# Copying two PSUM banks with one ScalarE instruction, from tiles two banks wide and four deep

## The chip, the cores and the metric

The kernel runs on one core of one Trainium2 chip. The metric is the device time of one execution in microseconds, the median of several runs. In the profiles PE is TensorE (the matmuls), DVE is VectorE, ACT is ScalarE, SP is the engine whose queue issues the transfers, and "PEclk" is the granted TensorE clock. A profile's span is about 1.8 us shorter than the timed execution.

## The reference

```python
batch, m, k, n = 16, 512, 768, 1024
x: [batch, k, m] float32      y: [batch, k, n] float32

def reference(x, y):
    return np.einsum('bkm,bkn->bmn', x, y).astype(np.float32)
```

Sixteen products of a transposed 768x512 matrix with a 768x1024 one. Each batch reads 1536 KB of x and 3072 KB of y and writes 2048 KB.

## The kernel before

For each batch the kernel loads x and y in float32, casts both to bfloat16 on VectorE, multiplies in 48 matmuls of 128x512 (4 row blocks `mo`, 2 column halves `nt`, 6 steps `kt` over K), lets ScalarE copy each finished PSUM bank into an output tile, and stores a whole batch with one transfer. Loads and stores share one queue. A batch's store is issued four batches late (`LAG = 4`), behind the loads of a later batch, so that it never waits for its data in the middle of the kernel. The last batch loads y in two halves, and keeps all its accumulations open while it goes through K in two passes.

```python
o_pool = ctx.enter_context(tc.tile_pool(name="o_pool", bufs=5))
psum = ctx.enter_context(tc.tile_pool(name="psum", bufs=8, space=bass.MemoryType.PSUM))
LAG = 4
# ...
for b in range(B):
    # ... loads of xs and ys; halves = 2 for the last batch, else 1
    if b >= LAG:
        store(b - LAG)
    # ... casts to x_sb, y_sb
    for h in range(halves):
        for mo in range(MT):
            for nt in range(NT):
                if h == 0:
                    ps[mo, nt] = psum.tile([P, NF], FP32, name="ps")
                for kt in range(h * KT // halves, (h + 1) * KT // halves):
                    mm(ps[mo, nt], x_w, y_sb, kt, mo, nt)
                if h == halves - 1:
                    nc.scalar.copy(o_sb[:, mo, nt * NF:(nt + 1) * NF], ps[mo, nt][:])
for b in sorted(o_tiles):      # the last four stores
    store(b)
```

Of the kernel before, what the change touches and what calls it, by code (L numbers as in the profile page):

```python
# [1 line left out]

_os.environ.setdefault("NEURON_RT_ULTRASERVER_MODE", "4")

# [1 line left out]

# [4 lines left out]


@with_exitstack
def kernel(
    ctx: ExitStack,
    tc: tile.TileContext,
    x: bass.AP,
    y: bass.AP,
    out: bass.AP,
):  # L20
    nc = tc.nc
    P = 128
    FP32 = mybir.dt.float32
    BF16 = mybir.dt.bfloat16

    B, K, M = x.shape
    _, _, N = y.shape
    KT = K // P
    MT = M // P
    NF = 512  # L30
    NT = N // NF



    x_v = x.rearrange("b (p ko) m -> b p ko m", ko=KT)
    y_v = y.rearrange("b (p ko) n -> b p ko n", ko=KT)
    o_v = out.rearrange("b (p mo) n -> b p mo n", mo=MT)

    xs_pool = ctx.enter_context(tc.tile_pool(name="xs_pool", bufs=2))
    ys_pool = ctx.enter_context(tc.tile_pool(name="ys_pool", bufs=2))  # L40
    x_pool = ctx.enter_context(tc.tile_pool(name="x_pool", bufs=2))
    y_pool = ctx.enter_context(tc.tile_pool(name="y_pool", bufs=2))
    o_pool = ctx.enter_context(tc.tile_pool(name="o_pool", bufs=5))
    psum = ctx.enter_context(tc.tile_pool(name="psum", bufs=8, space=bass.MemoryType.PSUM))
    LAG = 4
    KH = KT // 2
    o_tiles = {}

    def load(dst, src, rows):
        nc.sync.dma_start(dst, src)  # L50

    def store(b):
        nc.sync.dma_start(o_v[b], o_tiles.pop(b)[:])

    def mm(ps, x_w, y_sb, kt, mo, nt):
        nc.tensor.matmul(ps[:], x_w[:, kt, mo], y_sb[:, kt, nt * NF:(nt + 1) * NF],  # L56
                         start=(kt == 0), stop=(kt == KT - 1))

    with tc.manual_schedule():

        for b in range(B):
            xs = xs_pool.tile([P, KT, M], FP32, name="xs")
            ys = ys_pool.tile([P, KT, N], FP32, name="ys")
            halves = 2 if b == B - 1 else 1

            load(xs[:], x_v[b], 1)
            for h in range(halves):
                ks = slice(h * KT // halves, (h + 1) * KT // halves)
                load(ys[:, ks], y_v[b, :, ks], 1)

            if b >= LAG:
                store(b - LAG)
            x_sb = x_pool.tile([P, KT, M], BF16, name="x_sb")
            y_sb = y_pool.tile([P, KT, N], BF16, name="y_sb")
            nc.vector.tensor_copy(x_sb[:], xs[:])  # L75
            for h in range(2):
                ks = slice(h * KH, (h + 1) * KH)
                nc.vector.tensor_copy(y_sb[:, ks], ys[:, ks])  # L78
            x_w = x_sb[:].rearrange("p k (j mo) -> p k mo j", mo=MT)
            o_sb = o_pool.tile([P, MT, N], FP32, name="o_sb")  # L80
            o_tiles[b] = o_sb
            ps = {}


            for h in range(halves):
                for mo in range(MT):
                    for nt in range(NT):
                        if h == 0:
                            ps[mo, nt] = psum.tile([P, NF], FP32, name="ps")
                        for kt in range(h * KT // halves, (h + 1) * KT // halves):  # L90
                            mm(ps[mo, nt], x_w, y_sb, kt, mo, nt)
                        if h == halves - 1:
                            nc.scalar.copy(o_sb[:, mo, nt * NF:(nt + 1) * NF], ps[mo, nt][:])  # L93
        for b in sorted(o_tiles):
            store(b)


# [1 line left out]
_INS = ['x', 'y']  # L99
_OUTS = [((16, 512, 1024), 'float32')]  # L100


# [23 lines left out]
```

## Time and profile before

The time was 262.4 us in three runs.

| What | Before |
|---|---|
| span of the profile | 260.5 us |
| share of the 16 DMA engines used by the one queue | 98.4% |
| TensorE / VectorE / ScalarE busy | 73% / 32% / 29% |
| rate in the middle, 95 to 220 us | 431 GB/s |
| last copy ends | 245.65 us |
| DMA engines stay full until about | 256 us |

The lines behind this table are shown and read in the prediction.

### The profile page before, as it was taken

The page shows a single profiled execution, that of the slowest core. Times are in us where ns is not written, and L with a number is a line of the kernel's source. Part 1 is how long each engine was busy: PE and PEld are TensorE (multiplying, and loading weights), DVE is VectorE, ACT ScalarE, POOL GpSimd, SP SyncE. Part 2 cuts the span into 40 slices and gives each one's busy share as a digit, 9 for nine tenths or more (in the row PEclk, how much of TensorE's full clock was granted, in tenths as well). Part 3 has the DMA queues.
Part 4 walks back from the last instruction along what each step waited for, and adds up shares of the span by engine and source line. Part 5 has one row for each costly group of instructions (what it writes and reads, how often), then busy time and mean ns, then how long its engine had stood idle before and what let it go on. Part 6 is the DMA issues. An engine that isn't in the chain of part 4 may idle for free.

```text
span 260.5 us, 1879 instructions
## 1 busy us (share of the span) xinstructions
PE 191.3 (73%) x768; PEld 89.3 (34%) x768; DVE 83.1 (32%) x48; ACT 76.4 (29%) x129; POOL 0.2 (0%) x4
## 2 busy tenths in 40 slices
PE   0049999897939959688496966969789395899600
PEld 0014555453513514334142432434335142355200
DVE  0271633525222252322524214252132522252000
ACT  1003444442421403324032330323314043141600
POOL 0000000000000000000000000000000000000000
PEclk9999999999985977979898896797979889799955
DMA  7999999999999999999999999999999999999994
GB/s 279 434 434 411 445 423 436 426 387 420 446 416 442 423 422 455 409 440 418 438 435 415 453 418 431 423 428 449 410 443 421 426 445 407 431 430 430 435 428 201
DMA packets 7065, 109.18 MB, mean 419 GB/s; under 512 B 784, under 2 KB 784, under 8 KB 784
## 3 DMA queue, kind: packets, MB, share of 16 engines
q1 hardware_dynamic: 7056, 109.06, 98.4%
q8 instruction: 6, 0.10, 0.1%
q14 instruction: 3, 0.02, 0.0%
HBM read 75.50 MB, written 33.55 MB: 419 GB/s over the span
## 4 chain that ended last, share of the span: by engine, by line
DMA 74%; DVE 11%; PE 8%; issue 0%; ACT 0%; SPq 0%; DVEq 0%
DMA ys<-in_y_dram 74%; DVE y_sb L78 11%; PE ps L56 8%; ACT o_sb L93 0%; SPq L50 0%; DVEq L78 0%
## 5 line engine op out<-in xcount | busy, mean ns | idle before, releaser
L56 PE MATMUL ps<-y_sb,x_sb 128*128 128x512 bf16 x768 | 191.3, 412 | 53.8 <-DVE y_sb L78 53.8
L56 PEld LDWEIGHTS <-x_sb 128*128 128x128 bf16 x768 | 89.3, 118 | 155.2 <-issue 45.9
L93 ACT COPY o_sb<-ps 128x512 f32<-128x512 f32 x128 | 75.1, 587 | 168.6 <-PE ps L56 168.2
L78 DVE CAST y_sb<-ys 128x3072 bf16<-128x3072 f32 x32 | 55.0, 1757 | 87.4 <-DMA ys<-in_y_dram 87.4
L75 DVE CAST x_sb<-xs 128x3072 bf16<-128x3072 f32 x16 | 28.2, 1760 | 66.6 <-DMA xs<-in_x_dram 60.4
L93 ACT ACT_TABLE_LOAD x1 | 1.3, 1283 | 0.7 <-PEq L110 0.7
L110 POOL MEMSET const-bfloat16-1.0<- 128x1 bf16 x1 | 0.1, 101 | 0.0
L110 POOL MEMSET const-uint8-127<- 128x1 uint8 x1 | 0.1, 101 | 0.0
L110 POOL MEMSET const-float32-0.0<- 128x1 f32 x1 | 0.1, 98 | 0.2 <-issue 0.2
L110 POOL MEMSET const-float32-1.0<- 128x1 f32 x1 | 0.1, 98 | 0.0
## 6 DMA issues: line engine op xcount, KB each, us to landing
ys<-in_y_dram SPq DMA_DIRECT2D x15, 3072.0 KB, 28.1
out_dram<-o_sb SPq DMA_DIRECT2D x16, 2048.0 KB, 32.6
xs<-in_x_dram SPq DMA_DIRECT2D x16, 1536.0 KB, 29.7
ys<-in_y_dram SPq DMA_DIRECT2D x2, 1536.0 KB, 26.1
```

Of the source, the lines that this page charges most:

```text
L56: nc.tensor.matmul(ps[:], x_w[:, kt, mo], y_sb[:, kt, nt * NF:(nt + 1) * NF], start=(kt == 0), stop=(kt == KT - 1))
L75: nc.vector.tensor_copy(x_sb[:], xs[:])
L78: nc.vector.tensor_copy(y_sb[:, ks], ys[:, ks])
L93: nc.scalar.copy(o_sb[:, mo, nt * NF:(nt + 1) * NF], ps[mo, nt][:])
L110: nc = _bacc.Bacc("TRN2", target_bir_lowering=False, num_devices=1)
```

## The change

The intent is to pay the fixed part of a ScalarE instruction once for two banks. A PSUM tile becomes two banks wide, the pool four deep instead of eight (the same eight banks), and 64 copies of 1024 columns take the place of 128 copies of 512. The rest of the diff takes small helper functions apart and changes no instruction; it is cut here.

```diff
-    psum = ctx.enter_context(tc.tile_pool(name="psum", bufs=8, space=bass.MemoryType.PSUM))
+    psum = ctx.enter_context(tc.tile_pool(name="psum", bufs=4, space=bass.MemoryType.PSUM))
 ...
                 for mo in range(MT):
+                    if h == 0:
+                        ps[mo] = psum.tile([P, NT, NF], FP32, name="ps")
                     for nt in range(NT):
-                        if h == 0:
-                            ps[mo, nt] = psum.tile([P, NF], FP32, name="ps")
                         for kt in range(h * KT // halves, (h + 1) * KT // halves):
-                            mm(ps[mo, nt], x_w, y_sb, kt, mo, nt)
-                        if h == halves - 1:
-                            nc.scalar.copy(o_sb[:, mo, nt * NF:(nt + 1) * NF], ps[mo, nt][:])
+                            nc.tensor.matmul(
+                                ps[mo][:, nt], x_w[:, kt, mo],
+                                y_sb[:, kt, nt * NF:(nt + 1) * NF],
+                                start=(kt == 0), stop=(kt == KT - 1))
+                    if h == halves - 1:
+                        nc.scalar.copy(o_sb[:, mo].rearrange("p (t f) -> p t f", f=NF), ps[mo][:])
```

More of the change, by code (lines that the diff above doesn't have):

```diff
@@ L47 @@
     o_tiles = {}
-    def load(dst, src, rows):
-        nc.sync.dma_start(dst, src)
     def store(b):
-        nc.sync.dma_start(o_v[b], o_tiles.pop(b)[:])
-    def mm(ps, x_w, y_sb, kt, mo, nt):
-        nc.tensor.matmul(ps[:], x_w[:, kt, mo], y_sb[:, kt, nt * NF:(nt + 1) * NF],
-                         start=(kt == 0), stop=(kt == KT - 1))
+        o_sb = o_tiles.pop(b)
+        nc.sync.dma_start(o_v[b], o_sb[:])
     with tc.manual_schedule():
@@ L64 @@
             halves = 2 if b == B - 1 else 1
-            load(xs[:], x_v[b], 1)
+            nc.sync.dma_start(xs[:], x_v[b])
             for h in range(halves):
                 ks = slice(h * KT // halves, (h + 1) * KT // halves)
-                load(ys[:, ks], y_v[b, :, ks], 1)
+                nc.sync.dma_start(ys[:, ks], y_v[b, :, ks])
             if b >= LAG:
```

## The prediction

> **What bounds the kernel now.** I read the page first, then the chain of waits, the timeline of the end and of one middle batch, the windows over the last microseconds, and the waits of the DMA queue. The first question is which resource has no holes.
>
> ```profile
> PE   0049999897939959688496966969789395899600
> ACT  1003444442421403324032330323314043141600
> PEclk9999999999985977979898896797979889799955
> DMA  7999999999999999999999999999999999999994
> ...
> q1 hardware_dynamic: 7056, 109.06, 98.4%
> ...
> DMA ys<-in_y_dram 74%; DVE y_sb L78 11%; PE ps L56 8%; ACT o_sb L93 0%; SPq L50 0%; DVEq L78 0%
> ```
>
> From the page: the DMA row is 9 in every slice except the first and the last, and the one queue accounts for 98.4% of what 16 engines could do. The chain of work that ended last is 74% the y load and only a rounded 0% ScalarE's copy. TensorE has holes, and ScalarE, the engine that the change relieves, is never above six tenths.
>
> The size of a period fits. A batch moves 1536 KB of x, 3072 KB of y and 2048 KB of output, 6656 KB or 6.82 MB. In the timeline the y loads of successive batches are issued at 127.86, 143.68 and 159.56 us, 15.85 us apart. 6.82 MB in 15.85 us is 430 GB/s, which is what the windows view shows for the long middle stretch (95 to 220 us: 431 GB/s at full DMA share). So the middle of the kernel runs at the rate of the transfers. All 109.06 MB at 430 GB/s would be 253.6 us. The span is 260.5 us; the rest is the start, the ragged end of the last store (below), and slightly slower stretches.
>
> Next, does anything wait for ScalarE?
>
> ```profile
> ACT o_sb L93 <- PE ps L56: 168.2, 121, 17.4
> DVE y_sb L78 <- DMA ys<-in_y_dram: 87.4, 17, 6.8
> DVE x_sb L75 <- DMA xs<-in_x_dram: 60.4, 14, 7.1
> PE ps L56 <- DVE y_sb L78: 53.8, 25, 16.2
> ```
>
> In this list of waits (total us, times, longest) ScalarE waits for TensorE 121 times; TensorE waits for VectorE's cast, and VectorE for the loads. TensorE never appears as waiting for ScalarE. In the DMA queue's own list of waits ScalarE appears only three times, 32.2 us in all, before stores, and the timeline places these at the very end, where the last stores wait for the last batches to be computed.
>
> **What the Trainium skill says.** (1) "ScalarE: Activation LUTs", section What ACT_TABLE_LOAD costs: an activation without pointer operands costs 186 ns plus 0.833 ns per element. For 512 elements that gives 613 ns; the trace has 587 ns, 4% less. (2) "Perfetto Trace Analysis", section Optimizing Scalar/DVE Operations: grouping into larger operations helps throughput if the engine is saturated. At 29% busy, ScalarE is not, so the condition for a gain is missing. (3) "PSUM — Partial Sum Buffer", section PSUM bank collisions raise a hardware error: guard PSUM by bank; a reader and TensorE must not be in one bank together. A two-bank tile therefore keeps both banks from TensorE until the one wide copy is done; whether that costs time is worked out below. (4) "DMA: Bandwidth & Descriptors", Specifications: a fabric ceiling of 435 GB/s for the 16 engines. The steady 430 GB/s is 99% of it, which agrees, so no reordering of compute can make the middle faster.
>
> **The change, part by part.** The loads, casts, matmuls, stores and their order stay as they are: dropping the small helper functions changes no instruction, and the store pieces are still whole 2048 KB batches on the same queue. Two things move.
>
> ```profile
> L93 ACT COPY o_sb<-ps 128x512 f32<-128x512 f32 x128 | 75.1, 587 | 168.6 <-PE ps L56 168.2
> L56 PE MATMUL ps<-y_sb,x_sb 128*128 128x512 bf16 x768 | 191.3, 412 | 53.8 <-DVE y_sb L78 53.8
> ```
>
> *Fewer, wider copies.* 128 copies of 512 columns become 64 of 1024. Keeping the page's slope and taking the fixed part from the trace, 587 - 0.833 x 512 = 160 ns, a wide copy should take 160 + 853 = 1.01 us (estimate). ScalarE's copies fall from 75.1 to 64 x 1.01 = 65 us. These 10 us lie on an engine that stood idle 168.6 us waiting for TensorE, so they are worth nothing to the end.
>
> *Later start, later end of each copy.* The first bank of a pair now waits for the second. Within a batch the timeline has copies starting every 1.30 us, six matmuls of about 0.216 us each at full clock. So the first bank is read 1.30 us later, and the pair is finished 1.01 - 0.59 = 0.43 us later than its second bank was. In the middle this delays nothing: a batch's store is issued four batches, some 63 us, afterwards.
>
> *Coarser PSUM.* A tile is filled in 12 x 0.216 = 2.6 us and emptied in 1.0. Before TensorE needs it again it fills three others, 3 x 2.6 = 7.8 us. So about 6.8 us are to spare and TensorE should not stall. At a lower clock the filling is slower and the reserve larger. The last batch goes through K in two halves, so all four tiles are open at once. It starts at mo=0 after the preceding batch's tiles; its fourth tile is first written after 3 x 1.3 = 3.9 us, while the previous batch's last copy needs 1.0. In the second half TensorE needs six matmuls, 1.30 us, per pair and ScalarE 1.01, so ScalarE still keeps up.
>
> *The end.* This is the one place where the 0.43 us can reach the clock.
>
> ```profile
> 240.58 5.07 ACT L93 COPY o_sb<-ps 128x512 f32<-128x512 f32 x8 [5.29 <-PE ps L56]
> ...
> 246.00:248.00 2.00, 0.00 (x0) 0.00 (x0) 0.00 (x0) 0.00 (x0) 0.00 (x0) 0.88 1.05 451
> 248.00:250.00 2.00, 0.00 (x0) 0.00 (x0) 0.00 (x0) 0.00 (x0) 0.00 (x0) 0.50 0.98 418
> 250.00:252.00 2.00, 0.00 (x0) 0.00 (x0) 0.00 (x0) 0.00 (x0) 0.00 (x0) 0.50 0.98 418
> 252.00:254.00 2.00, 0.00 (x0) 0.00 (x0) 0.00 (x0) 0.00 (x0) 0.00 (x0) 0.50 1.05 451
> 254.00:256.00 2.00, 0.00 (x0) 0.00 (x0) 0.00 (x0) 0.00 (x0) 0.00 (x0) 0.50 0.96 410
> 256.00:258.00 2.00, 0.00 (x0) 0.00 (x0) 0.00 (x0) 0.00 (x0) 0.00 (x0) 0.50 0.44 188
> 258.00:261.00 3.00, 0.00 (x0) 0.00 (x0) 0.00 (x0) 0.00 (x0) 0.00 (x0) 0.50 0.06 27
> ```
>
> The last copy ends at 245.65 us and the last store is issued at 245.7. The last columns of the windows are DMA share and GB/s: the engines stay full until 256. Summing rate times width, 4.75 MB move after 246.0: 4.30 up to 256, then 0.38, then 0.08. The last store is 2048 KB, 2.10 MB. So some 2.66 MB of earlier stores were still ahead of it when it was issued, and at 430 GB/s that is **6.2 us of reserve** (estimate). A delay of 0.43 us uses 7% of it. The engines don't notice, and the end stays where it was.
>
> The sum: 0 from ScalarE's saved 10 us, 0 from PSUM, 0 from the tail, and the DMA's bytes are unchanged.
>
> **The rivals.** (a) *The tail shows*: if the last store ran alone, the end would move by 0.43 us, to 262.8 us. For it: the chain ends in a copy. Against it: the reserve of 2.66 MB. Even then it would be 0.2%. (b) *TensorE becomes starved of PSUM*: four deep instead of eight. If every one of 64 tiles stalled for the extra 0.43 us of copy, this would be 28 us on TensorE. Most of it would vanish into the 53.8 us in which TensorE waits for data, but from 18 to 51 us TensorE runs almost without a gap, three batches in about the time of their loads. Stalls there could delay the casts and hence the loads, by perhaps 12 x 0.43 = 5 us. Against it: 6.8 us to spare in every rotation. (c) *ScalarE was a hidden limit and the kernel gets faster*: if its saved 10 us counted, 252 us. Against it: no engine waits for it in the listed waits, and 252 us would be below the 253.6 us that the bytes need at 430 GB/s. (d) *The wide read is much slower than 1.01 us*, say 2 x 587 ns: then ScalarE is as busy as before and the tail is 0.59 us later, still inside the reserve.
>
> **Range and chances.** The point is the time before, 262.4 us. The three runs before span 0.5 us; another chip or session may shift a transfer-bound time by a few tenths of a per cent, a judgment and not a measurement. I take 261.4 to 263.6 us. For over 2% slower (267.6 us) rival (b) at its full size would be needed, 2%. For over 2% faster (257.2 us) the transfers would have to run at more than 430 GB/s, or the start and ragged end shrink, which the change doesn't touch: 1%.
>
> **What would show it.** In the changed kernel: 64 copies of 128x1024 near 1.01 us and about 65 us in all; TensorE's waits still put down to VectorE, none to ScalarE; the DMA row unchanged, the middle at 430 GB/s and a period of 15.85 us; the last copy ending about 0.4 us after TensorE's end plus 0.6, and the stores' end unchanged. It would be wrong if TensorE shows waits for ScalarE before y loads are issued later, if the last store finds the engines empty, or if the transfers' rate moves for a reason that the page doesn't show.

## More of the kernel before

The experiments were spread over three chips, each with the kernel before in the same rounds; there it took 262.00 to 262.25 us.

## The result, and the profile after

The changed kernel took 262.13 us (261.85 to 262.35, six runs), the kernel before 262.33 us (262.04 to 262.52, six runs). The ratio is 0.9993, with a 95% interval from 0.998 to 1.0006: the same. A ratio here is the mean time of one kernel's fast runs over that of the other's in the same rounds, so it isn't quite the ratio of the medians.

From the page of the changed kernel, the answers to the lines of before: two rows of the forty slices, the queue's share, the chain by line, and the two groups that changed.

```profile
ACT  1003343433321313314033330412404114131600
...
DMA  7999999999999999999999999999999999999995
...
q1 hardware_dynamic: 7056, 109.06, 98.5%
...
DMA ys<-in_y_dram 74%; DVE y_sb L70 11%; PE ps L83 8%; ACT o_sb L88 0%; SPq L59 0%; DVEq L70 0%
...
L83 PE MATMUL ps<-y_sb,x_sb 128*128 128x512 bf16 x768 | 189.9, 410 | 55.1 <-DVE y_sb L70 55.1
...
L88 ACT COPY o_sb<-ps 128x1024 f32<-128x1024 f32 x64 | 64.9, 1014 | 179.1 <-PE ps L83 179.1
```

The copies did become cheaper: 64 of 1014 ns, 64.9 us instead of 75.1. The idle time before them grew by about as much, from 168.6 to 179.1 us. TensorE still waits for VectorE's cast only, and the DMA row and the chain haven't moved. (The chain is followed back from the last copy, so the 14 us of stores after it are not part of it.) The saved time turned into more waiting on an engine that was already waiting.

At the end of the kernel, the timeline shows the last copy and the windows show the last transfers (the last two columns are DMA share and GB/s).

```profile
244.99 1.01 ACT L88 COPY o_sb<-ps 128x1024 f32<-128x1024 f32 x1 [0.28 <-PE ps L83]
```

```profile
254.00:256.00 2.00, 0.00 (x0) 0.00 (x0) 0.00 (x0) 0.00 (x0) 0.00 (x0) 0.50 1.03 442
256.00:258.00 2.00, 0.00 (x0) 0.00 (x0) 0.00 (x0) 0.00 (x0) 0.00 (x0) 0.50 0.52 221
258.00:261.00 3.00, 0.00 (x0) 0.00 (x0) 0.00 (x0) 0.00 (x0) 0.00 (x0) 0.50 0.04 16
```

The copy takes 1.01 us where it took 0.58, and ends at 246.00 us instead of 245.65 although TensorE finished 0.08 us earlier. The transfers still end where they did. The waits of the DMA queue show how the delay vanishes. This line is the time from the issue of the last store until it landed (us in total, times, longest), first for the kernel before, then for the changed one.

```profile
SPq L121 <- DMA out_dram<-o_sb: 13.4, 1, 13.4
```

```profile
SPq L116 <- DMA out_dram<-o_sb: 13.0, 1, 13.0
```

The last store was issued 0.35 us later and its wait became 0.4 us shorter. It had been standing in line behind earlier stores, and now it stands there for less time. The first experiments test this reading.

### The profile page after: what moved, and what is told of

The parts are those of the page before. It is cut to its first block, busy times and chain, and to the rows that moved or that the text cites. A ratio compares the mean times of both kernels' runs of the same rounds, so it can differ in the third digit from the quotient of the medians.

```text
span 260.4 us, 1815 instructions
## 1 busy us (share of the span) xinstructions
PE 189.9 (73%) x768; PEld 89.1 (34%) x768; DVE 83.1 (32%) x48; ACT 66.2 (25%) x65; POOL 0.2 (0%) x4
## 3 DMA queue, kind: packets, MB, share of 16 engines
q1 hardware_dynamic: 7056, 109.06, 98.5%
## 4 chain that ended last, share of the span: by engine, by line
DMA 74%; DVE 11%; PE 8%; ACT 0%; issue 0%; SPq 0%; DVEq 0%
DMA ys<-in_y_dram 74%; DVE y_sb L70 11%; PE ps L83 8%; ACT o_sb L88 0%; SPq L59 0%; DVEq L70 0%
## 5 line engine op out<-in xcount | busy, mean ns | idle before, releaser
L88 ACT COPY o_sb<-ps 128x1024 f32<-128x1024 f32 x64 | 64.9, 1014 | 179.1 <-PE ps L83 179.1
```

Source lines behind the costliest of these rows:

```text
L88: nc.scalar.copy(o_sb[:, mo].rearrange("p (t f) -> p t f", f=NF), ps[mo][:])
```

## The experiments

My theory: the bytes at 430 GB/s set the time; ScalarE, the depth of PSUM and the last copy all have room. Rivals: the end follows the last copy; the coarser tiles cost what the wider copies save, so that two real effects cancel; ScalarE counts after all, but a wide copy isn't really cheaper. Where an experiment differs from the changed kernel, its edit is shown against that one, unless said otherwise.

### Later last store

```diff
-                        nc.scalar.copy(o_sb[:, mo]..., ps[mo][:])
+                        for _ in range(5 if b == B - 1 and mo == MT - 1 else 1):   # 5, 9, 13
+                            nc.scalar.copy(o_sb[:, mo]..., ps[mo][:])
```

> The very last wide copy is done five times instead of once, so the last store is issued 4.1 us later. Theory (when the last store is issued, some 2.6 MB of earlier stores are still ahead of it, about 6 us of reserve): the time stays at 262.1, within 0.5 us. Rival (the end follows the last copy): 266.2 us.

> The last copy nine times, the last store 8.1 us later. Theory: the reserve of about 6 us is used up and the rest shows, with perhaps 1 us more for a store that starts on empty engines: 264 to 266 us. Rival (the end follows the last copy): 270.2 us. Rival (the end does not depend on the last copy at all): 262.1 us.

> The last copy thirteen times, the last store 12.2 us later. Theory: 4.1 us more than with nine copies, so 268 to 270 us, and the profile shows the DMA engines empty between the third last store and the last. Rival (the end follows the last copy all along): 274.3 us.

Measured: 262.24 us (ratio to the kernel before 1.0005), 262.57 us (1.002) and 266.51 us (1.0177). The extra copies took 4.2, 8.4 and 12.5 us. Four were hidden completely, eight nearly so, and of twelve about 4.4 us show. That rules out "the end follows the last copy", which asked for 266.2 us in the first of these, and it rules out that the end is independent of it. But the size was not what I had written: with eight, 264 us or more was expected, and with twelve 268 to 270.

The wait for the last store to land, with eight and then with twelve extra copies:

```profile
SPq L117 <- DMA out_dram<-o_sb: 5.8, 1, 5.8
```

```profile
SPq L117 <- DMA out_dram<-o_sb: 5.8, 1, 5.8
```

So a 2048 KB store that finds the engines free takes 5.8 us to land. In the changed kernel it took 13.0. The difference, **7.2 us**, is the reserve of the changed kernel, and 13.4 - 5.8 = 7.6 us is that of the kernel before. In the run with twelve extra copies the last store was issued here:

```profile
257.39 0.33 SPq L52 DMA_DIRECT2D out_dram<-o_sb  x1
```

It was out at 257.72 us instead of 246.36 (both ends of the issuing instruction), 11.36 us later; less 7.2, that is 4.2 us, and the span grew by 4.2 us, from 260.4 to 264.6. The 5.8 us of the run with eight thus foretell the run with twelve. With four, the last store was issued 3.5 us later than in the changed kernel and its wait fell to 9.7 us, 3.3 less, as for a store that stands in a line.

Why did adding up bytes give only 6.2? The windows of the run with eight extra copies, which issued its last store at 253.56 us:

```profile
250.00:252.00 2.00, 0.00 (x0) 0.00 (x0) 0.00 (x0) 1.94 (x3) 0.00 (x0) 0.50 0.75 320
252.00:253.00 1.00, 0.00 (x0) 0.00 (x0) 0.00 (x0) 0.97 (x2) 0.00 (x0) 0.50 0.31 131
253.00:254.00 1.00, 0.00 (x0) 0.00 (x0) 0.00 (x0) 0.54 (x1) 0.00 (x0) 0.50 0.04 16
...
258.00:259.00 1.00, 0.00 (x0) 0.00 (x0) 0.00 (x0) 0.00 (x0) 0.00 (x0) 0.50 1.23 524
259.00:261.00 2.00, 0.00 (x0) 0.00 (x0) 0.00 (x0) 0.00 (x0) 0.00 (x0) 0.50 0.00 0
```

The earlier stores don't end at one time. The share, a mean of the 16 engines, falls from 0.75 to 0.04 over some three microseconds. A store that comes after that ends sharply, at 524 GB/s and then nothing. No view lists the parts of a transfer, but the trace keeps the 16 times at which each transfer reports a part as landed, and they settle it. In the kernel before, the parts of the last store landed between 256.22 and 259.63 us, 3.4 us apart; in the run with eight extra copies they landed between 259.64 and 259.83, 0.2 us apart. Counted from the end of the issuing instruction, the mean part took 11.67 us in the kernel before and 5.87 when the store stood alone, 5.8 us more; the last part took 13.62 and 5.93, 7.7 us more. Adding up bytes gives about the first difference, and the end of the kernel needs the second. Which engines lag, and why, isn't shown.

The windows say the same. In the kernel before, 0.46 MB moved after 256 us in about 2.7 us; at 430 GB/s they would have taken 1.1. That 1.6 us is about the 1.4 by which the reserve was underrated.

### The tile shape alone

```diff
-                        nc.scalar.copy(o_sb[:, mo]..., ps[mo][:])
+                        for nt in range(NT):
+                            nc.scalar.copy(o_sb[:, mo, nt * NF:(nt + 1) * NF], ps[mo][:, nt])
```

> Half of the change alone: PSUM tiles two banks wide and four deep, but two copies of 512 columns from each. Theory: the tile shape costs nothing, 262.1 us within 0.5 us, copies 128 of 0.587 us, ScalarE busy 76 us. Rival (the coarser tiles cost something which the cheaper copies give back): over 262.6 us, and TensorE waits for ScalarE.

Measured: 262.38 us, ratio 1.0009 (0.9992 to 1.0026). The wide tiles by themselves cost nothing that these runs could resolve, so no gain and loss are cancelling each other. But ScalarE was busy for 70.1 us, not 76. The timeline of its copies shows why:

```profile
134.43 1.08 ACT L89 COPY o_sb<-ps 128x512 f32<-128x512 f32 x2 [1.85 <-PE ps L83]
137.02 1.08 ACT L89 COPY o_sb<-ps 128x512 f32<-128x512 f32 x2 [1.51 <-PE ps L83]
```

Two copies in a row take 1.08 us, while one takes 0.59: the second starts about 0.1 us before the first has ended. Against 1.08 us, a wide copy of 1.01 saves only some 0.06 us, not the 0.16 us of a whole fixed part. This asked for a test with ScalarE as the bound.

### Half of ScalarE's time, and all of it

First twice the wide copies, as a load test.

```diff
+                        for _ in range(2):
                             nc.scalar.copy(o_sb[:, mo]..., ps[mo][:])
```

> Every wide copy twice: ScalarE busy about 130 us instead of 66, half of the span. Theory (ScalarE is hidden behind the transfers): 262.1 us within 0.6 us. Rival (ScalarE's time counts, so the change should have brought something): some 10 us or more slower for 64 us of added work.

Measured: 262.22 us, ratio 1.0005 (0.999 to 1.002), with ScalarE 130.7 us busy:

```profile
PE 187.8 (72%) x753; PEld 88.8 (34%) x768; DVE 83.1 (32%) x48; ACT 130.7 (50%) x129; POOL 0.2 (0%) x4
```

Adding 64 us to ScalarE costs nothing, so ScalarE has that much room, and a gain from taking 10 away is not to be expected.

Then six times, once in the changed kernel and once in the kernel before.

> Every wide copy six times, so that ScalarE is the bound: 384 copies of 1.01 us are 389 us, or 353 us if copies that follow each other at once overlap by 0.09 us; with the start and the last store 380 to 425 us. It is the partner of the narrow kernel with six copies each. Theory (the change makes evacuation cheaper by about 0.16 us per pair, hidden so far): this is faster than its partner by over 8%. Rival (a wide copy is worth no more than two narrow ones when they follow each other at once): the two are within 2%.

> The kernel before with every narrow copy six times: 768 copies of 0.587 us are 451 us, or 379 us if copies that follow each other at once overlap by 0.09 us; with the start and the last store 405 to 485 us. Theory: slower than its wide partner by 8 to 15%. Rival: within 2% of it.

Measured: 428.32 us and 489.12 us, both some 4 us above the ranges expected; by these medians the narrow form is 14.2% slower, inside the 8 to 15% expected. Now TensorE waits for ScalarE, 153.5 and 194.9 us. But this pair overstates the gain, as the timelines of the wide and of the narrow copies show:

```profile
199.81 12.38 ACT L89 COPY o_sb<-ps 128x1024 f32<-128x1024 f32 x12
```

```profile
199.94 12.54 ACT L94 COPY o_sb<-ps 128x512 f32<-128x512 f32 x21
```

The wide copies follow each other at 12.38 / 12 = 1.03 us and the narrow ones at 12.54 / 21 = 0.60 us, with no overlap at all. Each of these copies writes the place that the one before has just written, and the trace shows what that does to the program: 320 of the 384 wide copies and 640 of the 768 narrow ones wait on a semaphore that only the copies themselves raise. In the kernel with narrow copies on wide tiles the second copy of a pair shows no such wait. The trace doesn't keep the value that is waited for; that it is the copy just before is argued from the spacing. So I repeated the test with copies that write different places.

```diff
+    scr = [s_pool.tile([P, NT, NF], FP32, name=f"scr{i}") for i in range(2)]
 ...
+                        for r in range(6):
+                            dst = (o_sb[:, mo]... if r == 5 else scr[r % 2][:])
+                            nc.scalar.copy(dst, ps[mo][:])
+        # narrow partner: for nt in range(NT): nc.scalar.copy(dst[:, nt], ps[mo][:, nt])
```

> ScalarE made the bound again with six wide copies of each PSUM tile, but now successive copies write different places (two scratch tiles in turn, the output last), so that none has to wait for the one before. Partner: the narrow form below. If copies overlap by about 0.1 us when they are independent, 384 copies cost 0.91 to 0.92 us each, 351 us, and the time is near 390 us; if not, 428 us as in the first six-copy kernel.

> The same, with two copies of 512 columns in the place of each wide one, from the same two-bank tiles. In the kernel with narrow copies on wide tiles two narrow copies in a row took 1.07 us, not 1.18. If that overlap holds for all of them and for wide copies too, 768 copies at about 0.49 us are 374 us and this is 5 to 8% slower than its wide partner: the saving of the change is some 0.06 us per pair. Rival (the whole 0.16 us of fixed part is saved): 13 to 15% slower, as with the first six-copy pair.

Measured: 387.58 and 412.67 us; the narrow form is 6.5% slower. The first line of each page, wide and then narrow:

```profile
PE 216.8 (56%) x768; PEld 93.6 (24%) x768; DVE 81.8 (21%) x48; ACT 353.5 (92%) x385; POOL 0.2 (0%) x4
```

```profile
PE 224.1 (55%) x768; PEld 94.3 (23%) x768; DVE 81.8 (20%) x48; ACT 377.8 (92%) x769; POOL 0.2 (0%) x4
```

Less 1.3 us for the table load, 384 wide copies took 352.2 us, 0.917 us each, and 768 narrow ones 376.5 us, 0.490 us each. Both are 0.097 us shorter than the single copies (1.014 and 0.587): only the places written had changed, and the overlap was back (many of these copies wait on that semaphore too, so it must be for an earlier copy). A pair costs 0.980 us narrow and 0.917 wide. So the change does make evacuation cheaper, by 0.063 us per pair where ScalarE never pauses. In this kernel that would be 64 x 0.063 = 4.0 us (an estimate from these two runs) even if ScalarE were the bound, and not the 10 us by which its busy time fell.

### The depth of PSUM

```diff
-    psum = ... bufs=4 ...
+    psum = ... bufs=2 ...                 # then bufs=1
-            for h in range(halves):       # computing only; loads stay in halves
+            for h in range(1):            # the last batch in one pass over K
```

> Two PSUM tiles of two banks instead of four, and the last batch computed in one pass over K (with two tiles it can't be kept open in halves). Theory: TensorE fills the other tile in 2.6 us while one is emptied in 1.0, so no stall. The last batch's matmuls can't start before its second half is cast only for the second half of each group, and so end up to 5 us later, inside the reserve of about 6 us: 262.1 us, at most 263.5. Rival (depth matters): TensorE waits for ScalarE and the time is over 264 us.

> One PSUM tile of two banks, so TensorE can't fill while ScalarE empties: the wait that rival (b) of the prediction feared, on purpose. A tile then takes 2.6 us of matmuls, 1.01 us of copy and some tenths for the two hand-overs, 3.9 us, 15.6 us for a batch, where the loads alone need 11 us and loads with stores 15.85. Theory: TensorE waits for ScalarE before nearly all of the 64 tiles, the first batches fall behind their loads, and the time is 266 to 300 us. If even this stays at 262, PSUM depth has no bearing on this kernel at all.

Measured: two tiles 262.06 us, ratio 0.9996 (0.998 to 1.0012), and TensorE waits for VectorE alone. One tile: 274.36 us, ratio 1.0471. There TensorE does wait for ScalarE, and the waits and the last windows show where it lands.

```profile
PE ps L83 <- ACT o_sb L88: 69.8, 63, 1.1
```

```profile
225.00:235.00 10.00, 6.70 (x31) 3.25 (x30) 1.51 (x1) 3.04 (x3) 0.00 (x0) 1.00 1.01 430
...
250.00:262.00 12.00, 8.65 (x38) 4.31 (x38) 0.00 (x0) 3.04 (x3) 0.00 (x0) 1.00 0.42 176
```

Before 63 of the 64 tiles TensorE waits 1.1 us for the copy. From the first matmul at 16.5 us to the end of the last copy at 265.4 us a tile takes 3.89 us, and the chain of this page is 65% TensorE and 24% ScalarE: their taking turns now sets the length. A batch of four tiles takes 15.6 us, just under the 15.85 us of its transfers, so the DMA engines stay full until 240 us, though the loads are issued late (the seventh x load at 65.44 us instead of 54.07, the seventh y load at 68.78 instead of 64.16). Then the loads and the stores that can be issued are done, and the engines idle while TensorE works off the last batches. The last batch's single pass isn't to blame, as the kernel with two tiles has it too. So the stall on PSUM shows at the end of this kernel, not in its middle. It takes a pool of one tile to bring it about; two are as good as four.

### Fewer bytes

Odd batches from 1 to 13 load only the first half of y and cast it twice.

```diff
+            half = b % 2 == 1 and b < B - 1
 ...
+                if half:
+                    ks = slice(0, KH)
                 nc.sync.dma_start(ys[:, ks], y_v[b, :, ks])
 ...
-                nc.vector.tensor_copy(y_sb[:, ks], ys[:, ks])
+                src = slice(0, KH) if half else ks
+                nc.vector.tensor_copy(y_sb[:, ks], ys[:, src])
```

> The changed kernel with the same matmuls, casts and copies, but in the seven odd batches from 1 to 13 only the first half of y is loaded and cast twice (the result is wrong on purpose). 7 x 1536 KB = 11.0 MB less to move, 25.6 us at 430 GB/s. Theory (the bytes are the bound and nothing else is near it): 236 to 243 us, the upper end if the early batches, which then load faster than TensorE's 10.4 us each, leave the DMA engines waiting. Rival (TensorE or ScalarE is close behind the transfers): over 250 us.

Measured: 236.67 us, 25.5 us below the changed kernel's 262.13 and 25.3 below the kernel before in the same rounds (262.00), where 25.6 were worked out. Matmuls, casts and copies were the same in number. The page:

```profile
DMA  6999999999999999999999999999999999999994
...
q1 hardware_dynamic: 7056, 98.04, 98.3%
```

The DMA row is as full as ever and the span shrank with the bytes. This shows that the transfers are the bound: what was taken from them came off the time in full, within the scatter of the runs, and what was taken from ScalarE came off not at all.

No run pointed to a version that beats both kernels by more than their noise, so none was built.

## Why the prediction was right

- **The bound.** 430 GB/s and 109.06 MB were said to set the time. The experiment with fewer bytes agrees within the scatter of the runs, 25.3 to 25.5 us against 25.6. That 430 GB/s is 99% of the ceiling which the prediction quotes is an agreement of two numbers; no run tests what sets this rate.
- **The wide copy.** 1.01 us was estimated, 1.014 measured; 65 us in all estimated, 64.9 measured. That excludes the fourth rival, a wide read as long as two narrow ones.
- **ScalarE's saved time is worth 0.** Right for the reason given: doubling its work changes nothing either. What the prediction called "its saved 10 us" in its third rival was overstated as a possible gain, since copies that follow each other at once overlap by 0.097 us. By the estimate above it would have been 4.0 us.
- **PSUM.** No stall was predicted, and TensorE's list of waits has none. The reserve turned out so ample that half the depth does as well. The second rival's idea of how a stall would hurt, through late loads in the first batches, was half right with one tile: x and y loads were issued up to 11.4 and 4.6 us late, but the DMA engines had work all the while, and the loss came at the end.
- **The tail.** The step "0.43 us later, inside the reserve" was right. The term that was mis-sized is the reserve: 6.2 us by summing bytes, 7.6 measured. The sum took the mean of the 16 engines, while the end is set by the part that lands last, 3.4 us after the first one in the kernel before.
- **Rivals.** The tail showing, TensorE starved, ScalarE as a hidden limit: each had an experiment in which it would have appeared, and appeared only after its reserve had been taken away on purpose.

The time itself, 262.13 against 262.4 us, lies within the scatter of the runs.

## What to carry to other kernels

Before making an engine's work cheaper, find out whether anything waits for that engine; if the list of waits doesn't name it as a releaser of the bound, the saved time only lengthens its idle time. Here a delay just before the last transfer was free as long as earlier transfers were queued ahead of it, and the wait for that transfer to land, less the time that it takes alone, was the reserve. Price the merging of instructions by their spacing when they follow each other at once, not by the length of one that stands alone.

## What the Trainium skill lacked or had wrong

- "ScalarE: Activation LUTs", What ACT_TABLE_LOAD costs: the slope holds (1014 - 587 = 427 ns for 512 more elements, 0.834 ns each). The fixed part was 160 ns for these copies out of PSUM, not 186; the page doesn't say for which memory its figure is. The overlap of about 93 ns between copies in a row was 97 ns. The page doesn't say that a program can lose it: copies that write the same place as the one before carried a semaphore wait, and their spacing was 1.03 and 0.60 us in the first six-copy pair, against 0.917 and 0.490 us.
- "Perfetto Trace Analysis", Matmul Optimizations: the advice to use all 8 PSUM banks had no effect here. Two tiles of two banks, half of PSUM, took 262.06 us, and only one tile (274.36 us) was slower. That isn't an error of the page, as TensorE is not the bound in this kernel.
- No page gives a size for how far apart the 16 parts of a transfer end (it would belong to "DMA: Bandwidth & Descriptors"): 3.4 us for the last store of the kernel before, 0.2 us for one that stood alone. That made the reserve before the last store 7.6 us instead of 6.2.
